# Third chunk's loads behind the second chunk's norm, rotary splits written in runs, zeros from all partitions, scale sums and masks later: one encoder layer on one core

## The chip, the cores and the metric

The kernel runs on one core of one Trainium2 chip. The core has a matrix engine (TensorE, PE in the profile), a vector engine (VectorE, DVE), a scalar engine (ScalarE, ACT), GpSimd (POOL) and SyncE (SP), which here only issues transfers between the chip's memory and the core's on-chip buffers; GpSimd issues some transfers too. The metric is the device time of one launch in microseconds. The kernel before took 2810.66 us, the median of three runs (2803.78, 2810.66 and 2811.31).

## The reference

One layer of an encoder for 2048 tokens of width 1024: a normalised input is projected to queries, keys, values and a gated branch; banded attention at three dilations and a gated depthwise convolution run side by side; then cross-attention over 256 memory rows and a squared-ReLU MLP with 4096 hidden columns. All inputs are float32. Cut to what matters here:

```python
y = rmsnorm(h, norm_mix_g[l]) @ w_in[l]                    # 1024 -> 3*512 + 2*512
q = partial_rotary(y[..., 0:D_ATT].reshape(B, S, 8, 64))   # first 16 of 64 columns turned
k = partial_rotary(y[..., D_ATT:2 * D_ATT].reshape(B, S, 8, 64))
v = y[..., 2 * D_ATT:3 * D_ATT].reshape(B, S, 8, 64)
att = dilated_sliding_attention(q, k, v).reshape(B, S, D_ATT)
conv = conformer_conv(a, g, ...)                           # a * sigmoid(g), 31 taps, layernorm, silu
h = h + jnp.concatenate([att, conv], axis=-1) @ w_out[l]
...                                                        # cross-attention over mem
u = rmsnorm(h, norm_mlp_g[l]) @ w_up[l]
h = h + jnp.square(jax.nn.relu(u)) @ w_down[l]
return rmsnorm(h, norm_final_g)
```

## The kernel before

**Stage 1** is the part that the prediction speaks of most: the norm of the input and the first projections, the first 400 us or so. A product of two float32 matrices is made of three products of halves: each operand is split into a high part in float16 (a cast) and a low part (the operand less its high part), and mm3 (L269 to L272) runs high times high, high times low and low times high into one accumulator. Weights are split the same way by scaled_split (L224 to L227): ACT multiplies by a power of two (L225) and casts (L226), and VectorE or GpSimd subtracts (L227).

The 2048 tokens come in four chunks of 512. For each chunk n, xprep (from L396) does the following. It loads four tiles of 128 tokens in two halves each (xn, eight transfers, from SP for chunks 0 and 1 and from GpSimd's queue for 2 and 3). ACT squares and sums them (sumsq, L381). Then rstd_col and newton_rsqrt make the reciprocal root: VectorE adds the epsilon (L243, st_v), GpSimd takes a power (L247, rsx), VectorE does one Newton step (L248 to L250). TensorE spreads the four columns to all partitions (rb, L255), and ACT copies that (rbs, L404). Then for each of eight column blocks TensorE transposes four tiles (xt, L409), VectorE copies the block and applies gain and norm (xv, L416), ACT casts it to the high half (xh, L417) and GpSimd subtracts for the low half (xl, L418). The un-normalised transpose goes to a scratch (xscr) through SP.

Beside it run the projections: glu_first (columns g and a of blocks 0 and 1, for chunks 0 and 1; sig at L667 is their gate, flo_a and flo_g the low halves of their weights), glu (the other blocks), lin_qk for queries and keys, and lin_v for values. lin_qk is called with "r" for the rotary columns, sixteen per head and eight heads, which are gathered in the order h, x, j (head, half, index) and written to the split weights in the order x, j, h; lraw_qr and lraw_kr are those weights in float32, lwhi and lwlo their halves (L818, L819). Their product is turned by VectorE and GpSimd (rope, sw) and split again (sth, stl, L878, L879). vscale loads each block of v's columns in two halves (vsq), squares them on ACT (L697), adds on GpSimd (L698, L699) and sums over partitions on TensorE (vss, L706), for a power-of-two scale. qkscale does the like for q and k with ACT (qks, L773). lin_v loads its weights (raw_v) and scales them (L729). memory transposes the 256 memory rows (mt, L440) and splits them on ACT and VectorE (mhi L446, mlo L447). edges writes zeros around v's scratch (vtok) and the convolution's scratch (uscr). Later, Matrices.back evicts a block of a matrix for the cross-attention out of the accumulators (eb, L578), scaled by a column.

**What sets the order.** The pieces are Python generators. weave steps a main one and, by a rate, side ones (L98); pinned and behind run a step as if it were issued right after an instruction that was recorded in the dictionary last under a name, by tc.issue_after (L78 to L96): "x1_7" is the cast of the second chunk's last high half, "xl0_7" the first chunk's last low half, "xs1" and "xs3" the last scratch store of chunks 1 and 3, "pe" the last matmul, "dve" the last recorded operation of VectorE. The framework then sorts each engine's queue by these positions. An engine runs its queue in order. SP's queue holds most transfers; each of its issues also waits, by a semaphore, for the transfer that was issued eight before it.

Of the kernel before, what the change touches and what calls it, by code (L numbers as in the profile page):

```python
# [12 lines left out]
F16 = mybir.dt.float16  # L13
BF16 = mybir.dt.bfloat16
I32 = mybir.dt.int32
AF = mybir.ActivationFunctionType
# [5 lines left out]
P = 128  # L22
S = 2048
D = 1024
H = 8
# [22 lines left out]
def hybrid_layer(ctx, tc, A, out):  # L48
# [7 lines left out]
    def dma(o, i, q=None):  # L56
        return (q or nc.sync).dma_start(o, i)  # L57
# [166 lines left out]
    def scaled_split(raw, c, hi, lo, eng):  # L224
        ACT.activation(raw, raw, AF.Copy, scale=c)  # L225
        last["split"] = ACT.copy(hi, raw)  # L226
        eng.tensor_tensor(lo, raw, hi, op=ALU.subtract)  # L227

# [17 lines left out]
    def newton_rsqrt(dst, v, t):  # L246
        POOL.tensor_tensor(dst, v, mhalf.to_broadcast([P, v.shape[1]]), op=ALU.pow)  # L247
        DVE.tensor_tensor(t, dst, dst, op=ALU.mult)  # L248
        DVE.scalar_tensor_tensor(t, t, -0.5, v, op0=ALU.mult, op1=ALU.mult)
        return DVE.scalar_tensor_tensor(dst, t, 1.5, dst, op0=ALU.add, op1=ALU.mult)  # L250
# [145 lines left out]
    def xprep(sp, n):  # L396
        xtiles(n)
        nat = [load_nat(sp, A["x"][0, 512 * n + P * j:512 * n + P * (j + 1), :], f"xn{n}_{j}", q=nc.gpsimd if n > 1 else None) for j in range(4)]
        yield
        r = yield from rstd_nat(sp, nat, f"x{n}", n == 1)  # L400
        rb = ps("c", f"rb{n}")
        last[f"rbt{n}"] = bcast_rows(rb, r, 4)
# [52 lines left out]
    class Matrices:  # L455
# [108 lines left out]
        def back(self, i):  # L564
# [5 lines left out]
            for mc in range(2):  # L570
# [6 lines left out]
                ev = zp.tile([P, 512], F32, tag=f"z{(2 * i + mc) % 8}", name=f"eb{h}{mc}{nh}")  # L577
                ACT.activation(ev, pt, AF.Copy, scale=rmem[:, mc:mc + 1])  # L578
                dma(bscr[4 * nh:4 * nh + 4, :, 2 * h + mc, :].rearrange("m p c -> p m c"),
# [110 lines left out]
    def vscale():  # L690

        for pr in range(4):
# [7 lines left out]
            yield  # L700
            yield
            with ExitStack() as st:
                after(st, "pe", "dve")
# [9 lines left out]
    def lin_v(hook):  # L713
# [4 lines left out]
        def load(e):  # L718
            raws[e] = wp.tile([P, 8, P], F32, tag="raw", name=f"raw_v{e}", bufs=2)
            with ExitStack() as st:  # L720
                after(st, "pe", "xs3")
                dma(raws[e], wcols(w_in, 2 * DATT + P * e))
# [23 lines left out]
        for t in range(4 * NG):  # L746
# [4 lines left out]
            for k in range(KC):  # L751
# [7 lines left out]
                                                   op1=ALU.subtract)  # L759
            dma(vtok[256 + P * t:256 + P * (t + 1)], st.rearrange("p h e -> p (h e)"))  # L760
            if t % 2:
# [36 lines left out]
    def lin_qk(isq, c):  # L798
# [5 lines left out]
        if c == "r":  # L804
# [9 lines left out]
            for x in range(2):  # L814
                rv = raw.rearrange("p k (h x j) -> p k h x j", x=2, j=8)[:, :, :, x, :]
                hv = hi[:, :, x * 64:(x + 1) * 64].rearrange("p k (j h) -> p k h j", h=H)
                lv = lo[:, :, x * 64:(x + 1) * 64].rearrange("p k (j h) -> p k h j", h=H)
                ACT.copy(hv, rv)  # L818
                DVE.tensor_tensor(lv, rv, hv, op=ALU.subtract)  # L819
# [97 lines left out]
    def edges():  # L917
        zrow = wp.tile([16, 1, VR], F16, tag="raw", name="zrow", bufs=2)
        DVE.memset(zrow, 0.0)
        zb = zrow.to_broadcast([16, 16, VR])  # L920
        for t0 in (0, 256 + S):
            dma(vtok[t0:t0 + 256].rearrange("(q x) e -> q x e", q=16), zb)
        for c in range(4):
            dma(uscr[c][:, 0:15], zero[:, 0:15])
            dma(uscr[c][:, 15 + S:2080], zero[:, 0:17])

    with ExitStack() as st:
# [40 lines left out]
        next(x1)  # L968
        next(four)
        early01 = (0, 1)  # L970
        units = [four] + [u for c in range(2, 4) for u in glu(c, early01)]
# [15 lines left out]
        mem = memory(sp)  # L987
        later = pinned(chain(xprep(sp, 2), islice(mem, 1), xprep(sp, 3), mem), "x1_7", "xl0_7")
        qks = pinned(qkscale(), "x1_7", "xs1")
# [22 lines left out]
    with ExitStack() as st0:  # L1012
        after(st0, "pe", "xs3")
        dma(mask, A["masks"])
# [1028 lines left out]
```

## Time and profile before

The profile is of one execution, taken by the hardware profiler.

| what | value |
|---|---|
| median of three runs | 2810.66 us (2803.78 to 2811.31) |
| the profiled execution's own time | 2811.16 us |
| its span in the profile | 2809.4 us |
| mean granted clock of TensorE | 0.989 |
| transfers | 535.67 MB, 191 GB/s over the span |

The span is what the engines' records cover; the execution's own time is what the runs are compared by. "Busy" is time inside instructions. Idle time is put down to the instruction that ended it: "[3.86 <-DVE rsx L250]" says that the engine stood for 3.86 us ahead of this instruction, and that the last thing it waited for was VectorE's line 250. The granted clock is what the throttle gave TensorE, 1.00 being full speed. A name such as rsx or xh stands for a buffer, and a line "xh<-xv" for writing the one from the other; a number in a buffer's name is left out there.

### The profile page before, as it was taken

Reading aid. Unit: us, or ns where it says so; the run is one execution under the profiler, and the core shown is the slowest. Engines: PE = TensorE matmul, PEld = TensorE weight load, DVE = VectorE, ACT = ScalarE, POOL = GpSimd, SP = SyncE. Lnnn points to the kernel's source line nnn. Section 1 sums busy time; section 2 is a strip of 40 time slices with the busy share of each in tenths; the row PEclk is TensorE's granted clock in tenths of the full one; section 3 lists DMA queues with packets and bytes.
Section 4 is the critical chain, followed back from the end, with each engine's and each line's share of the span. In section 5 each row is a group of like instructions: output and inputs, shape, how many; then the busy total and the mean of one; then the engine's idle time right before and its main releaser. Section 6 shows DMA issues by size and latency. Waiting matters only on the chain.

```text
span 2809.4 us, 40570 instructions
## 1 busy us (share of the span) xinstructions
PE 2695.4 (96%) x14783; PEld 2074.4 (74%) x14783; DVE 1901.4 (68%) x3477; ACT 1271.7 (45%) x2170; POOL 587.9 (21%) x807
## 2 busy tenths in 40 slices
PE   7979999889999999999999999999999999999998
PEld 4434448776778788788788788887887788878877
DVE  5548826665689876568986478666475776566765
ACT  6742316655545333434554443454344444444435
POOL 6445403543202122300111201121010122100000
PEclk9989999999999999999999999999999999999999
DMA  6775437887835666767467867774544554584553
GB/s 237 206 196 116 133 117 203 237 243 200 270 114 178 200 218 217 241 215 216 137 187 224 251 209 216 234 231 138 170 128 131 184 196 149 179 295 153 167 184 105
DMA packets 459815, 535.67 MB, mean 191 GB/s; under 512 B 98172, under 2 KB 329200, under 8 KB 459616
## 3 DMA queue, kind: packets, MB, share of 16 engines
q1 hardware_dynamic: 420992, 406.52, 48.4%
q0 software_dynamic: 36752, 123.06, 12.5%
q10 hardware_dynamic: 1872, 3.52, 0.3%
q8 instruction: 116, 1.90, 0.3%
q14 instruction: 83, 0.68, 0.1%
HBM read 384.46 MB, written 148.52 MB: 190 GB/s over the span
## 4 chain that ended last, share of the span: by engine, by line
PE 65%; DMA 10%; issue 9%; DVE 7%; ACT 4%; SPq 3%; POOL 3%; POOLq 0%; ACTq 0%; DVEq 0%
PE b L1741 5%; PE dn L270 4%; PE dn L271 4%; PE dn L272 4%; PE up L270 3%; PE up L272 3%; PE up L271 3%; SPq L57 3%; PE lin L270 2%; PE lin L271 2%; PE lin L272 2%; PE pt L1029 2%; PE s L1222 1%; PE x L271 1%; PE x L270 1%
## 5 line engine op out<-in xcount | busy, mean ns | idle before, releaser
L287 DVE SCALAR_TENSOR_TENSOR cacc<-cu,cwu,cacc 128x512 f32<-128x512 f32 x480 | 391.7, 818 | 6.2
L1023 ACT ACTIVATE sm<-sm,o 128x256 f32<-128x256 f32 (+1 forms) x384 | 160.0, 467 | 109.6 <-DVE o L1022 109.5
L270 PE MATMUL dn<-hhh,whi_d 128*128 128x512 f32 x512 | 201.9, 404 | 3.0 <-ACT hhh L1577 1.7
L270 PE MATMUL up<-mh,whi_u 128*128 128x512 f32 x512 | 203.9, 398 | 0.0
L271 PE MATMUL dn<-hhl,whi_d 128*128 128x512 f32 x512 | 200.0, 393 | 0.8 <-DVE hhl L1578 0.8
L272 PE MATMUL up<-mh,wlo_u 128*128 128x512 f32 x512 | 200.0, 391 | 0.0
L271 PE MATMUL up<-ml,whi_u 128*128 128x512 f32 x512 | 199.7, 390 | 0.0
L272 PE MATMUL dn<-hhh,wlo_d 128*128 128x512 f32 x512 | 198.9, 391 | 0.0
L1022 DVE CUSTOM_DVE_ANT_0 sm<-s,mask 128x256 f32<-128x256 f32 (+1 forms) x384 | 126.8, 374 | 35.8 <-PE s L1222 16.1
L1033 DVE TENSOR_TENSOR pl<-pt,ph 128x512 f16<-128x512 f32 x160 | 109.6, 686 | 48.6 <-ACT ph L1032 48.1
L247 POOL TENSOR_TENSOR nr<-st_v,mhalf 128x4 f32<-128x4 f32 x12 | 13.5, 1126 | 597.3 <-DVE st_v L243 597.3
L1592 DVE TENSOR_TENSOR h<-h,dn 128x512 f32<-128x512 f32 x128 | 86.3, 683 | 70.1 <-PE dn L272 69.5
L1032 ACT CAST ph<-pt 128x512 f16<-128x512 f32 x160 | 92.5, 578 | 79.3 <-PE pt L1029 78.5
L270 PEld LDWEIGHTS dn<-hhh,whi_d 128*128 128x128 f32 x512 | 95.3, 188 | 22.4 <-ACT hhh L1577 3.5
L272 PEld LDWEIGHTS up<-mh,wlo_u 128*128 128x128 f32 x512 | 96.1, 188 | 20.4
L272 PEld LDWEIGHTS dn<-hhh,wlo_d 128*128 128x128 f32 x512 | 96.2, 188 | 20.2
L271 PEld LDWEIGHTS dn<-hhl,whi_d 128*128 128x128 f32 x512 | 96.4, 188 | 19.4 <-DVE hhl L1578 1.7
L271 PEld LDWEIGHTS up<-ml,whi_u 128*128 128x128 f32 x512 | 96.3, 188 | 18.6
L270 PEld LDWEIGHTS up<-mh,whi_u 128*128 128x128 f32 x512 | 96.2, 188 | 18.6
L270 PE MATMUL o<-cath,whi_o 128*128 128x512 f32 x256 | 102.6, 402 | 5.3 <-ACT whi_o L261 4.6
L270 PE MATMUL x<-pth,whi_b 128*128 128x512 f32 x256 | 100.4, 398 | 2.4 <-ACT xp L1501 1.4
L270 PE MATMUL xs<-whi_a,yh 128*128 128x512 f32 x256 | 102.4, 401 | 0.0
(631 smaller groups left out, 7995.0 us busy)
## 6 DMA issues: line engine op xcount, KB each, us to landing
raw_u<-in_w_up_dram SPq DMA_DIRECT2D x64, 512.0 KB
raw_d<-in_w_down_dram SPq DMA_DIRECT2D x64, 512.0 KB
k<-kscr SPq DMA_DIRECT2D x32, 640.0 KB
raw_a<-ascr SPq DMA_DIRECT2D x32, 512.0 KB
raw_b<-bscr SPq DMA_DIRECT2D x32, 512.0 KB
lou<-wlo_u POOLq DMA_DIRECT2D x32, 512.0 KB, 5.5
lod<-wlo_d POOLq DMA_DIRECT2D x32, 512.0 KB, 5.8
wlo_u<-lou SPq DMA_DIRECT2D x32, 512.0 KB
```

Source lines behind the costliest of these rows:

```text
L57: return (q or nc.sync).dma_start(o, i)
L270: PE.matmul(o, lh, rh, start=first, stop=False)
L271: PE.matmul(o, lh, rl, start=False, stop=False)
L272: last["pe"] = PE.matmul(o, ll, rh, start=False, stop=end)
L287: DVE.scalar_tensor_tensor(acc, u[:, t:t + 512], cwu[:, c, t:t + 1], acc, op0=ALU.mult, op1=ALU.add)
L1022: last["dve"] = DVE.tensor_tensor_reduce(dst, so, mask[:, 256 * m:256 * m + nk], 1.0, 3e38, ALU.add, ALU.min, mn)
L1023: last["act"] = ACT.activation(dst, dst, AF.Exp, bias=mn, scale=-1.0)
L1029: last["pe"] = PE.transpose(pt[:, j, :], sm[:, j, :], ident)
L1032: ACT.copy(ph, pt)
L1033: DVE.tensor_tensor(pl, pt, ph, op=ALU.subtract)
L1592: last["dve"] = DVE.tensor_tensor(hs[m], hs[m], pt, op=ALU.add)
L1741: PE.matmul(o, w[i][:, k, :], Y[b][q][k], start=first and k + x == 0, stop=k == 3 and x == 2, skip_group_check=not first)
```

## The change

Seven edits:

1. The generator that prepares chunks 2 and 3 and the memory (later) is pinned behind the second chunk's last cast, the low half flo of the a-columns of block 1, and the last matmul, where it was pinned behind "x1_7" and "xl0_7". scaled_split records that low half, and newton_rsqrt its power (this record is not used). For chunks 2 and 3 xprep has one step more between the norm and rb.
2. Of the sixteen evictions in Matrices.back, the eight with mc = 1 go from ACT to VectorE.
3. vscale has one step more between the additions on GpSimd and the matmuls.
4. raw_v's loads are pinned behind "xs1" instead of "xs3".
5. The split of the rotary columns runs over x, j, h instead of h, x, j, so that each write goes to 64 float16 values in a row, and the reads jump.
6. The rows of zeros for vtok are read from 128 partitions, two rows from each, instead of 16 partitions with sixteen rows from each.
7. The mask's load is pinned behind the store of v's tile 7 instead of "xs3".

```diff
@@ scaled_split, newton_rsqrt
-        eng.tensor_tensor(lo, raw, hi, op=ALU.subtract)
+        last["lo"] = eng.tensor_tensor(lo, raw, hi, op=ALU.subtract)
...
-        POOL.tensor_tensor(dst, v, mhalf.to_broadcast([P, v.shape[1]]), op=ALU.pow)
+        last["pow"] = POOL.tensor_tensor(dst, v, mhalf.to_broadcast([P, v.shape[1]]), op=ALU.pow)
@@ xprep, after r = yield from rstd_nat(...)
+        if n > 1:
+            yield
@@ Matrices.back
-                ACT.activation(ev, pt, AF.Copy, scale=rmem[:, mc:mc + 1])
+                if mc:
+                    DVE.tensor_scalar(ev, pt, rmem[:, 1:2], None, op0=ALU.mult)
+                else:
+                    ACT.activation(ev, pt, AF.Copy, scale=rmem[:, 0:1])
@@ vscale, ahead of the matmuls
             yield
             yield
+            yield
@@ lin_v, load
-                after(st, "pe", "xs3")
+                after(st, "pe", "xs1")
                 dma(raws[e], wcols(w_in, 2 * DATT + P * e))
@@ lin_v, store of tile t
-            dma(vtok[256 + P * t:256 + P * (t + 1)], st.rearrange("p h e -> p (h e)"))
+            v = dma(vtok[256 + P * t:256 + P * (t + 1)], st.rearrange("p h e -> p (h e)"))
+            if t == 7:
+                last["v7"] = v
@@ lin_qk, "r"
-                rv = raw.rearrange("p k (h x j) -> p k h x j", x=2, j=8)[:, :, :, x, :]
-                hv = hi[:, :, x * 64:(x + 1) * 64].rearrange("p k (j h) -> p k h j", h=H)
-                lv = lo[:, :, x * 64:(x + 1) * 64].rearrange("p k (j h) -> p k h j", h=H)
+                rv = raw.rearrange("p k (h x j) -> p k x j h", x=2, j=8)[:, :, x]
+                hv = hi[:, :, x * 64:(x + 1) * 64].rearrange("p k (j h) -> p k j h", h=H)
+                lv = lo[:, :, x * 64:(x + 1) * 64].rearrange("p k (j h) -> p k j h", h=H)
                 ACT.copy(hv, rv)
                 DVE.tensor_tensor(lv, rv, hv, op=ALU.subtract)
@@ edges
-        zrow = wp.tile([16, 1, VR], F16, tag="raw", name="zrow", bufs=2)
+        zrow = wp.tile([P, 1, VR], F16, tag="raw", name="zrow", bufs=2)
         DVE.memset(zrow, 0.0)
-        zb = zrow.to_broadcast([16, 16, VR])
+        zb = zrow.to_broadcast([P, 2, VR])
         for t0 in (0, 256 + S):
-            dma(vtok[t0:t0 + 256].rearrange("(q x) e -> q x e", q=16), zb)
+            dma(vtok[t0:t0 + 256].rearrange("(q x) e -> q x e", q=P), zb)
@@ the weaving of stage 1
+        last["flo"] = last["lo"]
...
-        later = pinned(chain(xprep(sp, 2), islice(mem, 1), xprep(sp, 3), mem), "x1_7", "xl0_7")
+        later = pinned(chain(xprep(sp, 2), islice(mem, 1), xprep(sp, 3), mem), "x1_7", "flo", "pe")
@@ the mask's load
-        after(st0, "pe", "xs3")
+        after(st0, "pe", "v7")
         dma(mask, A["masks"])
```

What this does to the queues, at three places. First GpSimd's queue at the second chunk's norm, before (rsx is the power at L247; the xn rows are the loads of the third chunk):

```order
L418 TENSOR_TENSOR xl_0_391<-xv_7_619,xh_0_390 128x512
L57 DMA xn_0_0_911<-in_x_dram 128x512
L57 DMA xn_0_1_912<-in_x_dram 128x512
L57 DMA xn_1_0_915<-in_x_dram 128x512
L57 DMA xn_1_1_916<-in_x_dram 128x512
L57 DMA xn_2_0_919<-in_x_dram 128x512
L57 DMA xn_2_1_920<-in_x_dram 128x512
L57 DMA xn_3_0_923<-in_x_dram 128x512
L57 DMA xn_3_1_924<-in_x_dram 128x512
L247 TENSOR_TENSOR rsx_636<-st_v,mhalf 128x4
L227 TENSOR_TENSOR flo_a_675<-fraw_a_436,fhi_a_674 128x1024
L418 TENSOR_TENSOR xl_1_411<-xv_0_670,xh_1_410 128x512
```

And the same piece of GpSimd's queue with the change:

```order
L420 TENSOR_TENSOR xl_0_391<-xv_7_619,xh_0_390 128x512
L247 TENSOR_TENSOR rsx_636<-st_v,mhalf 128x4
L227 TENSOR_TENSOR flo_a_675<-fraw_a_436,fhi_a_674 128x1024
L57 DMA xn_0_0_911<-in_x_dram 128x512
L57 DMA xn_0_1_912<-in_x_dram 128x512
L57 DMA xn_1_0_915<-in_x_dram 128x512
L57 DMA xn_1_1_916<-in_x_dram 128x512
L57 DMA xn_2_0_919<-in_x_dram 128x512
L57 DMA xn_2_1_920<-in_x_dram 128x512
L57 DMA xn_3_0_923<-in_x_dram 128x512
L57 DMA xn_3_1_924<-in_x_dram 128x512
L420 TENSOR_TENSOR xl_1_411<-xv_0_670,xh_1_410 128x512
```

The power and the low half flo_a moved ahead of the eight loads, which now stand right before the second chunk's first low half.

Second, ACT's queue where the rotary columns are split, before (lraw_q is another weight tile, xh_3 the fourth chunk, mhi the memory's high half):

```order
L818 CAST lwhi_kr<-lraw_kr 128x8x8x8 x2
L417 CAST xh_3_1192<-xv_4_1449 128x512
L417 CAST xh_3_1192<-xv_5_1461 128x512
L417 CAST xh_3_1194<-xv_6_1473 128x512
L225 ACTIVATE lraw_q_1779<-lraw_q_1779,qkc 128x1024
L417 CAST xh_3_1194<-xv_7_1522 128x512
L818 CAST lwhi_qr<-lraw_qr 128x8x8x8 x2
L446 ACTIVATE mhi_1529<-mt_1533,gm 128x256
```

And with the change:

```order
L826 CAST lwhi_kr<-lraw_kr 128x8x64 x2
L419 CAST xh_3_1207<-xv_4_1449 128x512
L419 CAST xh_3_1207<-xv_5_1498 128x512
L419 CAST xh_3_1209<-xv_6_1510 128x512
L826 CAST lwhi_qr<-lraw_qr 128x8x64 x2
L225 ACTIVATE lraw_q_1779<-lraw_q_1779,qkc 128x1024
L419 CAST xh_3_1209<-xv_7_1571 128x512
L448 ACTIVATE mhi_1578<-mt_1582,gm 128x256
```

The casts of lwhi have another shape, and those of qr moved ahead of the scaling of lraw_q and of one cast of the fourth chunk.

Third, SP's queue behind the writes of zeros, before (vsq are the two halves of v's first block):

```order
L57 DMA rope_kr_1789<-in_rope_dram 128x512
L57 DMA lraw_k_1964<-in_w_in_dram 128x8x16
L57 DMA lraw_k_1964<-in_w_in_dram 128x8x48 x2
L57 DMA vsq_1824<-in_w_in_dram 128x4x128
L57 DMA lraw_k_1964<-in_w_in_dram 128x8x16
L57 DMA raw_v_2655<-in_w_in_dram 128x8x128
L57 DMA raw_v_2657<-in_w_in_dram 128x8x128
L57 DMA mask<-in_masks_dram 128x1664
L57 DMA vsq_1825<-in_w_in_dram 128x4x128
L57 DMA cu_0_1832<-uscr_70 128x542
```

And with the change:

```order
L57 DMA rope_kr_1789<-in_rope_dram 128x512
L57 DMA vsq_1824<-in_w_in_dram 128x4x128
L57 DMA lraw_k_1964<-in_w_in_dram 128x8x16
L57 DMA lraw_k_1964<-in_w_in_dram 128x8x48 x2
L57 DMA lraw_k_1964<-in_w_in_dram 128x8x16
L57 DMA vsq_1825<-in_w_in_dram 128x4x128
L57 DMA raw_v_2640<-in_w_in_dram 128x8x128
L57 DMA rope_kr_1834<-in_rope_dram 128x512
L57 DMA cu_0_1832<-uscr_70 128x542
```

The second vsq moved ahead of raw_v; one raw_v is gone from here to a place some 70 rows earlier (behind the first two qks loads), and the mask to one some 80 rows later.

## The prediction, made before the changed kernel was run

> **What bounds the kernel now.** I read the page first: engine totals, then the span in 40 slices.
>
> ```profile
> PE 2695.4 (96%) x14783; PEld 2074.4 (74%) x14783; DVE 1901.4 (68%) x3477; ACT 1271.7 (45%) x2170; POOL 587.9 (21%) x807
> PE   7979999889999999999999999999999999999998
> ```
>
> TensorE is busy for 96% of 2809.4 us, and its thin slices are the first and the third (70 us each), in stage 1. A saving must take idle time from TensorE, so I next asked for its busy time and granted clock by stretches (columns: stretch, its length, then busy us of PE, PEld, DVE, ACT, POOL with counts, the granted clock, DMA share, GB/s).
>
> ```profile
> 40.00:250.00 210.00, 184.09 (x857) 89.78 (x855) 118.64 (x188) 107.65 (x188) 104.00 (x104) 0.92 0.70 184
> 250.00:415.00 165.00, 165.00 (x770) 75.52 (x769) 106.41 (x137) 35.82 (x47) 54.54 (x73) 1.00 0.42 116
> 45.00:50.00 5.00, 4.41 (x15) 1.99 (x16) 1.78 (x5) 3.69 (x7) 1.17 (x2) 0.66 0.10 36
> 80.00:90.00 10.00, 8.23 (x27) 3.20 (x27) 2.87 (x6) 10.00 (x24) 6.94 (x5) 0.66 0.58 183
> 145.00:155.00 10.00, 7.13 (x27) 3.90 (x28) 6.56 (x11) 4.97 (x9) 5.96 (x14) 0.66 0.87 193
> 175.00:185.00 10.00, 8.64 (x27) 3.85 (x28) 2.61 (x4) 5.68 (x8) 7.96 (x7) 0.60 0.44 99
> 210.00:225.00 15.00, 11.64 (x44) 5.09 (x42) 14.89 (x14) 6.73 (x10) 12.83 (x14) 0.77 0.59 148
> ```
>
> From 250 to 415 us TensorE has no gap; from 40 to 250 it has 210 − 184.09 = 25.9 us of them, at a mean clock of 0.92. The timeline of TensorE says where (start, duration, instruction; in brackets the idle time before it and who ended it).
>
> ```profile
> 45.59 0.62 PE L255 MATMUL rb<-ident,rsx 128*128 128x128 f32 x4 [3.86 <-DVE rsx L250]
> 79.41 0.65 PE L255 MATMUL rb<-ident,rsx 128*128 128x128 f32 x4 [2.27 <-DVE rsx L250]
> 81.83 0.59 PE L270 MATMUL lin<-xh,lwhi_g 128*128 128x512 f16 x1 [1.77 <-ACT sig L667]
> 147.87 1.94 PE L440 MATMUL mt<-ident,mn 128*128 128x128 f32 x8 [5.52 <-DVE mlo L447]
> 176.25 1.01 PE L706 MATMUL vss<-ones,vsq 128*128 128x1 f32 x4 [6.15 <-POOL vsq L699]
> 208.57 0.38 PE L270 MATMUL lin<-xh,lwhi_k 128*128 128x512 f16 x1 [2.36 <-DVE rope_qr L866]
> 214.90 1.01 PE L706 MATMUL vss<-ones,vsq 128*128 128x1 f32 x4 [3.36 <-POOL vsq L699]
> ```
>
> These seven sum to 25.3 us. Behind the long ones the clock drops: what a stretch loses on top of its idle time is about (1 − clock) × busy time, so 0.34 × 4.41 = 1.5 us at 45, 0.34 × 8.23 = 2.8 at 80, 0.34 × 7.13 = 2.4 at 145, 0.40 × 8.64 = 3.4 at 175, 0.23 × 11.64 = 2.7 at 210: 12.8 us. So some 38 us in five places are on offer in stage 1, and each edit is weighed against the place it touches.
>
> **The change part by part.** I number the five places.
>
> **Place 1, the second chunk's norm (45.59).** What the late transposes waited for, on GpSimd and its neighbours:
>
> ```profile
> 36.58 3.76 POOL L57 DMA_DIRECT2D xn<-in_x_dram  x7
> 36.71 0.17 DVE L243 TENSOR_SCALAR st_v<-ssx 128x4 f32<-128x4 f32 x1
> 41.89 1.04 POOL L247 TENSOR_TENSOR rsx<-st_v,mhalf 128x4 f32<-128x4 f32 x1
> 38.59 1.05 ACT L226 CAST fhi_a<-fraw_a 128x1024 f16<-128x1024 f32 x1
> 42.91 2.11 POOL L227 TENSOR_TENSOR flo_a<-fraw_a,fhi_a 128x1024 f16<-128x1024 f32 x1
> 53.74 0.38 PE L271 MATMUL lin<-xl,lwhi_g 128*128 128x512 f16 x1
> 64.91 1.61 POOL L57 DMA_DIRECT2D xn<-in_x_dram  x3 [2.37 <-PE xt L409]
> ```
>
> The variance is there at 36.88, but the power at L247 begins at 41.89: eight load issues of the third chunk stand before it on GpSimd, 5 us. The changed kernel puts them behind the power and behind flo_a. The power can then run at 36.9 and rsx is ready about 5 us earlier, which covers the 3.86 us stall, and the 1.5 us of clock go with it: 5.3. What is late next: the eight issues (3.76/7 = 0.54 each, 4.3 in all) now stand between flo_a and the second chunk's first xl. flo_a would end near 41.8 (ACT's cast fhi_a ends at 39.64, then 2.11), the issues near 46.2, and the first xl near 47.3; its reader, at 53.74 now, comes about 6 us earlier, at 47.7. The cover is 0.4 us. I take **5.3**, bounds 0 (all given back) and 5.4.
>
> The rows give 0.54 us for each of these loads, at 36.58 and again at 64.91 (1.61/3), and the sum goes by that. [...]
>
> **Place 2, the third chunk's norm (79.41 and 81.83).** ACT's timeline:
>
> ```profile
> 73.65 0.63 ACT L773 ACTIVATE qks<-qks 128x512 f32<-128x512 f32 x1 [0.87 <-DMA qks<-in_w_in_dram]
> 81.10 0.68 ACT L667 ACTIVATE sig<-lin,wscl 128x512 f32<-128x512 f32 x1
> ```
>
> ACT's squares of the third chunk are mixed with squares of q and k columns that wait for their transfers, and behind them comes sig. In the changed order more of the chunk's squares precede the waiting ones, and one square, not eight, stands ahead of the cast and sig. The extra yield puts rb only two matmuls later. Of 2.27 + 1.77 + 2.8 = 6.8 I leave about 2 us of wait, since the loads start later too; a 2.36 us wait (208.57) is too short to have cost clock. I take **4.8**, bounds 0 and 6.8.
>
> **Place 3, rotary splits before mem's transposes (147.87).**
>
> ```profile
> 137.72 1.15 ACT L225 ACTIVATE lraw_q<-lraw_q,qkc 128x1024 f32<-128x1024 f32 x1 [2.35 <-DMA lraw_q<-in_w_in_dram]
> 139.28 4.71 ACT L818 CAST lwhi_qr<-lraw_qr 128x512 f16<-128x512 f32 x2
> 141.78 4.67 DVE L819 TENSOR_TENSOR lwlo_qr<-lraw_qr,lwhi_qr 128x512 f16<-128x512 f32 x2 [5.22 <-ACT lwhi_qr L818]
> 188.81 1.16 ACT L878 ACTIVATE sth_kr<-rope_kr,qkc 128x512 f16<-128x512 f32 x1
> 152.91 1.08 DVE L879 SCALAR_TENSOR_TENSOR stl_kr<-rope_kr,qkc,sth_kr 128x512 f16<-128x512 f32 x1 [1.04 <-ACT sth_kr L878]
> ```
>
> A cast that writes single f16 values 16 bytes apart takes 4.71/2 = 2.36 us, the subtraction 2.34. In the changed form writes run in 64s and only the reads jump. No row has this form; the nearest, also 512 elements a partition with strided f32 reads and f16 runs, are sth_kr at 1.16 and stl_kr at 1.08. Bounds 1.1 and 2.36; I take 1.15. The qr pair then costs 2.3 on each engine instead of 4.7, and its casts stand ahead of lraw_q instead of behind it, so that neither its 2.35 us wait nor its 1.15 us delays them: mlo can be 4.8 us earlier by the casts and some 3.5 by the order, against a stall of 5.52. With 2.4 of clock I take **8**, bounds 3 (if the casts cost what they did) and 8.
>
> **Place 4, the first sums of v's columns (176.25).** The chain of waits and SP's queue:
>
> ```profile
> 139.11 12.99 SPq L57 DMA_DIRECT2D uscr<-zero  x8
> 162.22 2.08 SPq L57 DMA_DIRECT2D raw_v<-in_w_in_dram  x2
> 164.35 1.16 SPq L57 DMA_DIRECT2D mask<-in_masks_dram  x1
> 165.61 7.74 DMA vsq<-in_w_in_dram
> 142.00:148.00 6.00, 0.48 (x3) 0.16 (x2) 5.85 (x6) 3.81 (x6) 0.11 (x1) 0.79 0.90 100
> 156.00:160.00 4.00, 4.00 (x20) 1.77 (x19) 0.00 (x0) 0.00 (x0) 0.00 (x0) 1.00 1.03 390
> ```
>
> The eight tiny zero transfers hold SP for 12.99 us, because an issue waits for the transfer eight before it and the two large writes of zeros (520 KB each, 16 partitions) move at 100 GB/s: 1.065 MB / 100 GB/s = 10.6 us. From 128 partitions they could move at the 390 GB/s seen at 156, 2.7 us; bounds 2.7 and 10.6, and I take the fast end, since wide reads are what reached 390. That brings SP forward by about 8 us. Behind it, one raw_v (512 KB), the other raw_v and the mask (832 KB) no longer stand ahead of the second vsq, whose issue at 165.61 and landing 7.74 later end the wait; it now follows lraw_k directly. I estimate landing at 152 to 156 on the old scale instead of 173.4, and the matmuls stand 24 matmuls (5.2 us) later on TensorE. Stall 6.15 and clock 3.4 could go whole; since lraw_k and the ropes remain ahead, I take **8** of 9.6, bounds 0 and 9.6.
>
> The rows leave open whether the 100 GB/s come from the few partitions or from writing the same zeros again and again. [...]
>
> **Place 5, 208.57 and 214.90.** The same chain one turn later: GpSimd works off what the late vsq had held up, and the rotary work and the second sums wait for it. These sums go from matmul 816 to 875 of the order, and their loads are ahead of time. Of 2.36 + 3.36 + 2.7 = 8.4 I take **6.5**, bounds 0 and 8.4.
>
> **The evictions of the matrices, and the loads made later.**
>
> ```profile
> L578 ACT ACTIVATE eb<-pb,rmem x16: 687/688/698, 684.6 to 722.1; 128x512 f32<-128x512 f32 x16
> 684.00:723.00 39.00, 29.62 (x163) 22.59 (x161) 13.42 (x30) 21.68 (x35) 15.90 (x21) 0.90 0.94 322
> L1022 DVE CUSTOM_DVE_ANT_0 sm<-s,mask x384: 273/415/426, 439.3 to 1869.4; 128x256 f32<-128x256 f32 x128, 128x128 f32<-128x128 f32 x64
> L729 DVE TENSOR_TENSOR raw_v<-raw_v,vbc x4: 1212/1214/1222, 294.6 to 318.2; 128x1024 f32<-128x1024 f32 x4
> ```
>
> Eight evictions of 0.688 us leave ACT for VectorE, 5.5 us, at about the same price. In the stretch where they lie ACT is busy 21.7 of 39 us and VectorE 13.4, but the DMA share is 0.94, so most of TensorE's gaps there are the transfers'. I take **1.2**, bounds −1 and +3. The mask is first read at 439.3, and its new place, behind the store of v's eighth tile, lies between the last of raw_v's products (318.2) and that, with the transfers at a share of 0.42 from 250 to 415: 0. raw_v is first read at 294.6; its early copy moves 512 KB ahead of q and k squares that place 2 has let wait, at most 2.2 us of transfers there, which is within that place's bounds.
>
> **Sum.** 5.3 + 4.8 + 8 + 8 + 6.5 + 1.2 = 33.8. Every stage-1 chain is tight, and what was hidden behind one stall stands bare when it goes: I take off 5, two new waits of the 2.4 us kind seen at 208.57. That leaves 29: 2811.16 − 29 = **2782 us**. The profiled execution lies 0.5 above the median of 2810.66 (2803.78 to 2811.31), so the sum needs no shift.
>
> **Rivals.** First, *the queue does not help*: the zeros stay slow, or vsq is late behind lraw_k all the same. For it: vsq took 7.74 us to land although only 256 KB, and the share is 1.03 already at 156. Against it: 1.35 MB leave its front. Then places 4 and 5 keep their 18 us and only two thirds of the rest stays, 5.3 + 4.8 + 8 + 1.2 − 2 = 17: **2794**. Second, *the change does nothing that can be told*: stalls move with the work, as each chain ends in the same matmuls; for it speaks that rb's second wait ends with ACT, which is busy 10.00 of 10 us at 80 to 90; against it, that there is no wait from 250 to 415 which could take them up. About 2808. Third, *slower*: GpSimd's eight issues at their new place take far longer than 0.54, and hold up both the second chunk's xl and the third chunk's loads. It decides from the point where the issues take the 0.4 us of cover plus the whole gain of 29, that is over 4.2 us each in place of 0.54. At 5 us each they take 40, 36 more than now: TensorE stands some 35 us and loses 2.8 of clock, against 29 gained: 38 − 29 = 9 slower, **2820**. The quoted rows speak against it, with 0.54 at both places.
>
> **How the numbers follow.** My forecast has 0.69, the queue's rival 0.20, no change 0.06, slower 0.05. About 0.3% (8.4 us) is what a measurement of this kernel can tell from no change; 2782 and 2794 are both beyond it, so faster 0.89, same 0.06, slower 0.05. The range: full removal of all bounds, 5.4 + 6.8 + 8 + 9.6 + 8.4 + 3 = 41, gives 2770 below; above, the first rival with place 2 gone too gives 17 − 4.8 = 12, 2799. So 2770 to 2799 holds some 8 in 10.
>
> **What would show it.** Place 1: the power starts within 1 us of st_v, and eight issues behind flo_a at about 0.54. Place 2: rb2's wait under 2.3, no sig wait. Place 3: casts of lwhi_qr near 1.15 us and no wait of mt on mlo. Place 4: SP's eight small zeros take some 4 us instead of 12.99, transfers near 390 GB/s, and vss waits for nothing. Place 5: no clock below 1.00 from 175 to 250. TensorE's idle time between 40 and 250 should fall from 25.9 to about 8 us. I am wrong if xl becomes the wait at 47, if the f16 casts stay above 2 us, so that ACT keeps place 3, or if vsq still lands last.

## The result, and the profile after

The changed kernel takes 2782.68 us, the median of six runs (2778.42 to 2786.64), beside 2810.98 us for six runs of the kernel before (2803.78 to 2817.11). The ratio is 0.990, with a 95% interval of 0.9882 to 0.9918: 23 to 33 us less. The profiled execution of the changed kernel took 2778.42 us, the lowest of its six; its span is 2776.6 us. It was a lucky one, and its stage 1 is the earliest of the three executions that are compared below.

Engine totals and the span in 40 slices, from the page of the changed kernel:

```profile
PE 2686.4 (97%) x14783; PEld 2073.0 (75%) x14783; DVE 1905.0 (69%) x3485; ACT 1261.7 (45%) x2162; POOL 588.0 (21%) x807
PE   7999999998999999999999999999999999999998
```

TensorE's busy time fell by 9 us too, with the same 14783 instructions; its mean granted clock is 0.993 where it was 0.989. The stretch that carried the sum, in the changed kernel, and two pieces of it that are used further on:

```profile
40.00:250.00 210.00, 201.87 (x989) 99.79 (x987) 139.20 (x210) 107.99 (x196) 120.75 (x128) 0.98 0.72 193
46.00:62.00 16.00, 16.00 (x89) 8.92 (x88) 9.07 (x18) 5.12 (x9) 11.00 (x13) 1.00 0.70 254
190.00:200.00 10.00, 10.00 (x42) 4.27 (x41) 9.82 (x11) 6.20 (x9) 9.57 (x10) 0.87 0.41 112
```

Idle time in these 210 us fell from 25.9 to 8.1 us. What the clock lost, (1 − clock) × busy time, fell from 0.08 × 184.09 = 14.7 to 0.02 × 201.87 = 4.0. Together 28.5 us. Now the first product of v's tiles, the first row of the stage in which TensorE has no gap, before and after:

```profile
330.44 0.38 PE L270 MATMUL v<-wvh,xh 128*128 128x512 f16 x1
```

```profile
301.89 0.38 PE L270 MATMUL v<-wvh,xh 128*128 128x512 f16 x1
```

That is 28.55 us earlier. The two executions differ by 32.7 us as a whole (2811.16 and 2778.42), so the other 4 us came behind this row, where stage 1 has no part. This row is the measure of the experiments: it holds what stage 1 gave and nothing of the noise behind it. One execution of each kernel stands behind the 28.55; over three executions of the changed stage 1, further on, it is 26.5, beside 28.3 for the medians.

Of the seven long waits three are left. TensorE's timeline of the changed kernel, the waits of more than 1 us between 40 and 250 us:

```profile
75.03 0.38 PE L270 MATMUL lin<-xh,lwhi_g 128*128 128x512 f16 x1 [3.81 <-ACT sig L672]
76.69 1.11 PE L255 MATMUL rb<-ident,rsx 128*128 128x128 f32 x4 [1.06 <-DVE rsx L250]
...
189.30 0.58 PE L270 MATMUL lin<-xh,lwhi_k 128*128 128x512 f16 x1 [2.30 <-DVE rope_qr L874]
```

The second chunk's rb, mt and vss no longer wait. The wait of lin on sig has doubled, from 1.77 to 3.81. The moved pieces at work, first on GpSimd, then on ACT, SP and TensorE:

```profile
36.78 1.03 POOL L247 TENSOR_TENSOR rsx<-st_v,mhalf 128x4 f32<-128x4 f32 x1 [0.31 <-DVE sqv_a L214]
39.53 2.13 POOL L227 TENSOR_TENSOR flo_a<-fraw_a,fhi_a 128x1024 f16<-128x1024 f32 x1 [1.72 <-ACT fhi_a L226]
41.60 4.32 POOL L57 DMA_DIRECT2D xn<-in_x_dram  x8
```

```profile
127.78 2.05 ACT L826 CAST lwhi_qr<-lraw_qr 128x512 f16<-128x512 f32 x2
129.51 6.15 SPq L57 DMA_DIRECT2D uscr<-zero  x8
144.34 0.63 ACT L702 ACTIVATE vsq<-vsq 128x512 f32<-128x512 f32 x1 [3.25 <-DMA vsq<-in_w_in_dram]
149.49 0.63 ACT L702 ACTIVATE vsq<-vsq 128x512 f32<-128x512 f32 x1 [0.50 <-DMA vsq<-in_w_in_dram]
160.57 0.50 PE L712 MATMUL vss<-ones,vsq 128*128 128x1 f32 x4
```

The power begins at 36.78 instead of 41.89, the eight issues take 0.54 us each at their new place, a cast takes 1.03 us, SP's eight small zeros 6.15, and the second vsq is squared at 149.49 where it landed at 173.35 before.

### The profile page after: what moved, and what is told of

It reads as the page before. It is cut to its first block, busy times and chain, and to the rows that moved or that the text cites. A ratio compares the mean times of both kernels' runs of the same rounds, so it can differ in the third digit from the quotient of the medians.

```text
span 2776.6 us, 40568 instructions
## 1 busy us (share of the span) xinstructions
PE 2686.4 (97%) x14783; PEld 2073.0 (75%) x14783; DVE 1905.0 (69%) x3485; ACT 1261.7 (45%) x2162; POOL 588.0 (21%) x807
## 4 chain that ended last, share of the span: by engine, by line
PE 69%; DMA 9%; issue 8%; DVE 7%; ACT 3%; POOL 3%; SPq 2%; ACTq 0%; POOLq 0%; DVEq 0%
PE b L1750 7%; PE dn L270 4%; PE dn L271 4%; PE dn L272 4%; PE up L270 3%; PE up L272 3%; PE up L271 3%; PE lin L270 2%; PE lin L272 2%; PE lin L271 2%; PE pt L1038 2%; SPq L57 2%; PE s L1231 2%; PE x L271 1%; PE x L270 1%
## 5 line engine op out<-in xcount | busy, mean ns | idle before, releaser
L247 POOL TENSOR_TENSOR nr<-st_v,mhalf 128x4 f32<-128x4 f32 x12 | 13.5, 1126 | 596.4 <-DVE st_v L243 596.4
L271 PE MATMUL o<-catl,whi_o 128*128 128x512 f32 x256 | 101.0, 395 | 1.7 <-DVE catl L1181 1.7
```

The costliest lines, as they stand in the source:

```text
L271: PE.matmul(o, lh, rl, start=False, stop=False)
```

## The experiments

Where a kernel undoes a part, it starts from the changed kernel; "alone" starts from the kernel before. The measure is the start of v's first product (330.44 before, 301.89 changed).

**How far one stage 1 differs from itself.** The changed kernel again, unaltered:

> The changed kernel once more, unaltered, as the measure for the others on the same chip. Its first profile had the lowest time of six, and the runs that share its stage 1 had v's first product at 306.0 and 306.2 instead of 301.9. If that profile was the odd one: v's first product at 304 to 307 and a wait of lin on sig of 4.2 to 5.2 us. If it was typical: 301 to 303. The ratio to the kernel before again 0.988 to 0.992.

```profile
77.03 0.59 PE L270 MATMUL lin<-xh,lwhi_g 128*128 128x512 f16 x1 [5.01 <-ACT sig L672]
191.13 0.38 PE L270 MATMUL lin<-xh,lwhi_k 128*128 128x512 f16 x1 [1.44 <-DVE rope_qr L874]
...
303.70 0.38 PE L270 MATMUL v<-wvh,xh 128*128 128x512 f16 x1
```

2784.31 us (2777.95 to 2790.89), ratio 0.9901 with 0.9881 to 0.9920. v's first product at 303.70, between my two guesses. A third execution of the same stage 1 comes from this edit, which undoes the evictions only:

```diff
-                if mc:
-                    DVE.tensor_scalar(ev, pt, rmem[:, 1:2], None, op0=ALU.mult)
-                else:
-                    ACT.activation(ev, pt, AF.Copy, scale=rmem[:, 0:1])
+                ACT.activation(ev, pt, AF.Copy, scale=rmem[:, mc:mc + 1])
```

> The changed kernel with all sixteen evictions on ACT. Stage 1 is the changed kernel's, so v's first product tells how far the same stage 1 differs from run to run: 301.9 to 304. From the first pb product to the last it took 34.9 us before and 34.4 after. If the evictions matter: 35 to 36 us. If the transfers set that stretch: 34.2 to 34.8.

It gave 306.18. So one stage 1 differs by 4.3 us between executions (301.89, 303.70, 306.18; mean 303.9), mostly in the wait on sig (3.81, 5.01, 4.73) and the waits from 160 to 230, and a difference of less than some 4 us between two single profiles is not told. The stretch of pb products took 33.6 us with all evictions on ACT (660.4 to 694.0), beside 34.4 and 33.9 in two executions of the changed kernel: no gain from moving them can be told. VectorE pays a little more for one than ACT:

```profile
L583 ACT ACTIVATE eb<-pb,rmem x8: 667/688/692, 653.5 to 684.7; 128x512 f32<-128x512 f32 x8
L581 DVE TENSOR_SCALAR eb<-pb,rmem x8: 750/751/752, 654.9 to 688.6; 128x512 f32<-128x512 f32 x8
```

(The columns are minimum, median and maximum in ns, and the first and last start.) The single time of this run, 2795.26, says little: from v's first product to pb's it took 354.2 us, where the other executions of the changed kernel and of its variants took 348 to 356.

**Place 1, undone and alone.**

```diff
@@ third chunk's pin undone
-        if n > 1:
-            yield
...
-        later = pinned(chain(xprep(sp, 2), islice(mem, 1), xprep(sp, 3), mem), "x1_7", "flo", "pe")
+        later = pinned(chain(xprep(sp, 2), islice(mem, 1), xprep(sp, 3), mem), "x1_7", "xl0_7")
```

> The changed kernel with the third chunk's loads pinned as before and without xprep's extra step. My theory of place 1: the eight load issues stand ahead of the power again, rb of the second chunk waits about 3.9 us and the clock drops behind it, so the first product of v's tiles, at 301.9 us in the changed kernel, starts 4 to 6 us later, at 306 to 308, less up to 1 us if place 2 gets better by its old order. The rival: the power's place is worth nothing, because the low half flo or the loads set the pace anyway; then 301.9 within 1 us.

TensorE's timeline of that kernel:

```profile
46.36 1.09 PE L255 MATMUL rb<-ident,rsx 128*128 128x128 f32 x4 [3.73 <-DVE rsx L250]
81.48 0.65 PE L255 MATMUL rb<-ident,rsx 128*128 128x128 f32 x4 [2.30 <-DVE rsx L250]
83.90 0.59 PE L270 MATMUL lin<-xh,lwhi_g 128*128 128x512 f16 x1 [1.77 <-ACT sig L670]
...
202.33 0.42 PE L270 MATMUL lin<-xh,lwhi_k 128*128 128x512 f16 x1 [3.87 <-DVE rope_qr L872]
```

v's first product at 315.89, 12.0 later than the mean of 303.9: more than place 1, and twice what was expected. The rb wait is back as foretold, the old form of place 2 with it (2.30 + 1.77), and the rotary products wait 1.43 us at 165 and 3.87 at 202. Idle time and clock together, place 1 lost 6.6 us (40 to 64 us), the rotary products 4 to 5 us more than in the three executions, and place 2 (64 to 100 us) about what it lost there, 6.9 beside 6.4 to 8.4. The mt wait did not return. The same edit alone, made on the kernel before:

> The kernel before with the third chunk's loads behind the second chunk's norm and xprep's extra step, and nothing else. Place 1 by my theory: the power at 36.8, no wait of rb on rsx at 41 to 46, eight issues of 0.54 us behind flo, xl ready in time. Place 2 by what the changed kernel showed: a wait of lin on sig of 3 to 5.5 us in place of 1.77. In sum v's first product 4 to 8 us before 330.4. The rival: the 5 us of place 1 stand at mlo or vss again, whose chains this doesn't touch, and v's first product is within 3 us of 330.4.

```profile
132.50 4.76 ACT L820 CAST lwhi_qr<-lraw_qr 128x512 f16<-128x512 f32 x2
...
76.62 0.59 PE L270 MATMUL lin<-xh,lwhi_g 128*128 128x512 f16 x1 [4.67 <-ACT sig L669]
141.28 1.06 PE L442 MATMUL mt<-ident,mn 128*128 128x128 f32 x8 [0.74 <-DVE mlo L449]
166.00 1.01 PE L708 MATMUL vss<-ones,vsq 128*128 128x1 f32 x4 [7.25 <-POOL vsq L701]
208.26 1.01 PE L708 MATMUL vss<-ones,vsq 128*128 128x1 f32 x4 [5.64 <-POOL vsq L701]
```

v's first product at 323.02, 7.4 earlier. Place 1 is cured (no wait of rb between 40 and 64 us), place 2 has the new long wait on sig, and place 3 is nearly cured as well (5.52 to 0.74) although the casts still take 2.38 us each: this edit is what moves lwhi_qr ahead of lraw_q on ACT. What was saved ahead of vss stands partly in front of it (6.15 to 7.25, 3.36 to 5.64).

**Place 3, the form of the rotary split, undone and alone.**

```diff
-                rv = raw.rearrange("p k (h x j) -> p k x j h", x=2, j=8)[:, :, x]
-                hv = hi[...].rearrange("p k (j h) -> p k j h", h=H)
+                rv = raw.rearrange("p k (h x j) -> p k h x j", x=2, j=8)[:, :, :, x, :]
+                hv = hi[...].rearrange("p k (j h) -> p k h j", h=H)
```

> The changed kernel with the rotary split's old form (h, x, j); every queue keeps its order. My theory of place 3, that the price of the casts counts: four casts near 2.36 us instead of 1.03, four subtractions near 2.34 instead of 1.0, mlo 3 to 5 us later, a wait of mt on mlo of 1 to 4 us, and v's first product 2 to 6 us later than 301.9. The rival, that the order of ACT's queue alone cured place 3: the casts cost 2.36 but no wait comes back, 301.9 within 1 us.

```profile
132.25 4.76 ACT L826 CAST lwhi_qr<-lraw_qr 128x512 f16<-128x512 f32 x2
...
141.00 1.06 PE L442 MATMUL mt<-ident,mn 128*128 128x128 f32 x8 [0.70 <-DVE mlo L449]
161.15 0.38 PE L270 MATMUL lin<-xh,lwhi_qr 128*128 128x512 f16 x1 [2.68 <-DVE rope_kr L874]
```

With the old form and the new order mt waits 0.70 us only, less than the 1 to 4 I gave. v's first product at 310.05, 6.1 later, comes with a wait of 2.68 us behind it, at a rotary product of q; with its clock that wait cost 4.3 us (150 to 180 us). So the form is worth something here too, at another place. And the new form with the old order:

> The kernel before with the rotary split in the new form and nothing else; ACT's queue keeps its old order, with the waiting lraw_q ahead of lwhi_qr. If the price of the casts is place 3: the casts take 1.03 us, mlo comes 3.5 to 5 us sooner, mt's wait falls from 5.52 to under 2, and v's first product is 4 to 8 us before 330.4. If the order is needed too (lraw_q's transfer holds the casts): a wait of 2.5 to 4.5 us stays and v's first product is 1 to 3.5 us before 330.4.

```profile
133.46 1.15 ACT L225 ACTIVATE lraw_q<-lraw_q,qkc 128x1024 f32<-128x1024 f32 x1 [2.12 <-DMA lraw_q<-in_w_in_dram]
135.03 2.03 ACT L818 CAST lwhi_qr<-lraw_qr 128x512 f16<-128x512 f32 x2
...
172.19 1.02 PE L706 MATMUL vss<-ones,vsq 128*128 128x1 f32 x4 [10.79 <-POOL vsq L699]
```

Here lraw_q still waits for its transfer ahead of the casts, and yet mt does not wait at all. v's first product at 323.72, 6.7 earlier, with vss's wait grown from 6.15 to 10.79. So the form and the order each cure place 3 without the other; with both, one of them is idle there.

**Place 4, the zeros, undone and alone, and from 32 partitions.**

```diff
-        zrow = wp.tile([P, 1, VR], F16, tag="raw", name="zrow", bufs=2)
+        zrow = wp.tile([16, 1, VR], F16, tag="raw", name="zrow", bufs=2)
...
-        zb = zrow.to_broadcast([P, 2, VR])
+        zb = zrow.to_broadcast([16, 16, VR])
```

> The changed kernel with the zeros written from 16 partitions; SP's order is kept. My theory of place 4: SP's eight small zeros take about 13 us instead of 6.15, vsq lands some 7 us later, and vss or the rotary products wait again, v's first product 3 to 8 us later than 301.9. The rival, that moving raw_v, the mask and vss out of the way was enough: vsq lands 7 us later too, but the sums were ready 8 us ahead of vss, so no wait and 301.9 within 1 us.

```profile
132.91 15.25 SPq L57 DMA_DIRECT2D uscr<-zero  x8
...
156.21 0.63 ACT L702 ACTIVATE vsq<-vsq 128x512 f32<-128x512 f32 x1 [11.76 <-DMA vsq<-in_w_in_dram]
160.87 1.15 ACT L225 ACTIVATE lraw_k<-lraw_k,qkc 128x1024 f32<-128x1024 f32 x1 [3.66 <-DMA lraw_k<-in_w_in_dram]
163.90 0.58 ACT L872 COPY sw_kr<-lin 64x512 f32<-64x512 f32 x1 [1.37 <-POOL vsq L703]
...
165.85 0.59 PE L270 MATMUL lin<-xh,lwhi_qr 128*128 128x512 f16 x1 [6.93 <-DVE rope_kr L874]
```

v's first product at 313.51, 9.6 later. The wait has another name: vss stands late enough on TensorE not to wait, but a rotary product waits 6.93 us for VectorE's rope_kr, which waits for ACT's copy sw_kr. ACT's rows show the link: it stands 11.76 us at the first square of vsq, whose load is late (3.25 in the changed kernel), then 3.66 at lraw_k (2.52 there), and sw_kr stands behind both on its queue. Only 1.37 us of sw_kr's delay is a wait for GpSimd's addition of vsq, as in the changed kernel (1.38); vsq and sw share one ring of buffers (t2), which would explain it, but no run tests that. The zeros alone, on the kernel before:

> The kernel before with the zeros read from 128 partitions and nothing else. If the zeros set place 4: SP's eight small zeros take about 6 us instead of 12.99, vsq lands some 7 us sooner, vss's 6.15 us wait goes nearly whole with its clock, and v's first product comes 6 to 10 us before 330.4. If raw_v and the mask ahead of vsq hold it anyway (1.35 MB, some 3.5 us at 390 GB/s): a wait of vss of 3 to 5 us stays, and v's first product is 1 to 4 us before 330.4.

```profile
138.95 5.72 SPq L57 DMA_DIRECT2D uscr<-zero  x8
...
200.97 0.59 PE L270 MATMUL lin<-xh,lwhi_k 128*128 128x512 f16 x1 [3.20 <-DVE rope_qr L866]
207.30 0.61 PE L706 MATMUL vss<-ones,vsq 128*128 128x1 f32 x4 [2.06 <-POOL vsq L699]
```

v's first product at 320.08, 10.4 earlier, the largest part of the three edits made alone, though not by more than single profiles differ. The first vss does not wait, with raw_v and the mask still ahead of the second vsq, so that the transfers in front of it are not what held it.

```diff
-        zrow = wp.tile([P, 1, VR], F16, tag="raw", name="zrow", bufs=2)
+        zrow = wp.tile([32, 1, VR], F16, tag="raw", name="zrow", bufs=2)
```

(and eight rows from each of them)

> The changed kernel with the zeros read from 32 partitions, eight rows from each. SP's eight small zeros took 12.99 to 15.25 us with 16 partitions and 6.15 with 128. If the number of partitions sets the rate (100 GB/s from 16, so some 200 from 32): 1.065 MB in 5.3 us instead of 10.6, the small zeros 7.5 to 10 us. If only the writing of the same lines counted, and the 128 were lucky: 12 to 15 us. If 32 are as good as 128: 6 to 7 us.

SP's row from 32 partitions, then windows in which the zeros are written, from 32 and from 128 (the last two columns are the transfer engines' share and the GB/s of all transfers in the window):

```profile
131.69 8.39 SPq L57 DMA_DIRECT2D uscr<-zero  x8
```

```profile
134.00:137.00 3.00, 3.00 (x17) 1.63 (x16) 1.84 (x4) 2.38 (x6) 1.14 (x2) 1.00 0.90 198
```

```profile
129.00:132.00 3.00, 3.00 (x17) 1.68 (x16) 1.89 (x2) 2.65 (x4) 0.42 (x2) 1.00 1.04 391
```

100 GB/s from 16 partitions, 198 from 32 and 391 from 128, at transfer shares of 0.90, 0.90 and 1.04. The same rows are written in all three, so the writing of the same zeros is not what set the rate. The last figure is an upper bound for the zeros: that window moved 1.17 MB, more than their 1.065. How often each partition is read changes along with their number (16, 8 and 2 rows from each), and no run separates the two. Twice the partitions gave twice the rate from 16 to 32, and four times as many, from 32 to 128, at most twice again. At 304.16 v's first product does not tell 32 partitions from 128.

**Place 2, which went the other way.** First the early raw_v, undone:

```diff
-                after(st, "pe", "xs1")
+                after(st, "pe", "xs3")
                 dma(raws[e], wcols(w_in, 2 * DATT + P * e))
```

> The changed kernel with raw_v's loads pinned behind the fourth chunk's stores as before. Place 2 went otherwise than I forecast: sig waits 3.8 us because ACT stood 3.1 us for the first q and k columns. Theory A: the early raw_v, 512 KB right behind the first two of these loads, shares the transfer engines with them; without it they land 1.5 to 3 us sooner, the wait of lin on sig falls under 2.5 us, and v's first product comes 1 to 3 us earlier than 301.9, less what raw_v costs at its old place. Theory B: they land late because SP issues them late and the fourth chunk's loads go beside them; raw_v has nothing to do with it, sig waits 3.5 to 4 us as before, and 301.9 within 1 us.

SP's and ACT's timelines in the changed kernel, and then in this one:

```profile
61.65 1.07 SPq L57 DMA_DIRECT2D qks<-in_w_in_dram  x2
...
68.58 0.63 ACT L781 ACTIVATE qks<-qks 128x512 f32<-128x512 f32 x1 [3.13 <-DMA qks<-in_w_in_dram]
74.30 0.68 ACT L672 ACTIVATE sig<-lin,wscl 128x512 f32<-128x512 f32 x1
```

```profile
62.13 2.54 SPq L57 DMA_DIRECT2D qks<-in_w_in_dram  x5
...
69.86 0.63 ACT L781 ACTIVATE qks<-qks 128x512 f32<-128x512 f32 x1 [3.93 <-DMA qks<-in_w_in_dram]
```

ACT stands 3 to 4 us at the first square of q and k with or without the early raw_v; v's first product at 306.00 lies within the spread of the changed kernel. So raw_v's place is worth nothing that can be told, there or further on. SP issues these loads at 61.65 in the one and 62.13 in the other, and ACT starts the square 7 to 8 us later (5.4 before). In seven executions, the changed kernel's two and five of its variants, lin's wait on sig is 0.6 to 0.7 us longer than ACT's stand at that square: 3.13 and 3.81 here, 4.40 and 5.01 in the changed kernel again, 4.60 and 5.21 with the zeros from 16 partitions. What lies behind ACT's standing square is the rest of the third chunk's squares, the cast and sig. The test is to take q's and k's squares out of that stretch:

```diff
-        weave(islice(steps, 34), (later, 0.4), (qks, 0.2))
+        weave(islice(steps, 10), (later, 0.4))
+        weave(islice(steps, 24), (later, 0.4), (qks, 0.283))
```

> The changed kernel with qkscale woven in from the eleventh step on, at a rate of 0.283 instead of 0.2 from the first, so that no square of q and k columns stands among the third chunk's squares on ACT. Theory B of place 2 (ACT stands 3 to 4.6 us for the first q and k columns, which land 7 us after their issue whether raw_v is early or not, and sig and the chunk's norm stand behind): the wait of lin on sig falls from 3.8 to 5.2 us to under 1.5, rb's is under 1.5, the clock holds in that stretch, and v's first product starts 3 to 6 us before 301.9 to 306; the median is 2 to 7 us under 2782.7. The rival: the fourth chunk's squares, which stand ahead of sig too, or the later scale of q and k wait in their place, and v's first product stays within 1.5 us of 301.9.

```profile
72.85 0.38 PE L270 MATMUL lin<-xh,lwhi_g 128*128 128x512 f16 x1 [0.45 <-ACT sig L672]
154.18 0.38 PE L270 MATMUL lin<-xh,lwhi_qr 128*128 128x512 f16 x1 [1.90 <-DVE rope_kr L874]
160.97 0.38 PE L270 MATMUL lin<-xh,lwhi_qr 128*128 128x512 f16 x1 [1.12 <-DVE rope_kr L874]
189.87 0.38 PE L270 MATMUL lin<-xh,lwhi_k 128*128 128x512 f16 x1 [2.84 <-DVE rope_qr L874]
```

The wait on sig is gone (0.45), although as many squares stand ahead of sig on ACT as in the changed kernel, eleven. So the standing at the load is the cause, and not the number of the squares. But v's first product stands at 302.62, 1.3 before the mean of 303.9: the rotary products wait 1.90 + 1.12 us where the changed kernel did not wait. Beside the changed kernel on the same chip:

> The kernel with q's and k's squares woven in from the eleventh step, beside the changed kernel on the same chip. Theory B of place 2: no wait of sig, v's first product 2 to 5 us ahead of the changed kernel's, and the ratio to the kernel before lower by 0.0007 to 0.002. The rival: what place 2 gives is taken by the rotary products' waits at 154 to 208, and the two ratios agree within 0.0005.

2781.11 us (2780.24 to 2782.68), ratio 0.9892 with 0.9874 to 0.9910; in its first run 0.9878 with 0.9853 to 0.9903. v's first product at 302.19. It is faster than the kernel before. That it beats the changed kernel, whose ratio measured beside it is 0.9901 with 0.9881 to 0.9920, is not told: the two intervals lie over each other. So the rival of both expectations, that other waits take what place 2 gives, can't be excluded, and the 3 to 6 us first expected did not come.

## Why the prediction was right, point by point

The forecast of 2782 us met 2782.68. The sum had 33.8 − 1.2 − 5 = 27.6 us for stage 1, and the trace shows 28.5 there (26.5 over three executions); TensorE's idle time between 40 and 250 us was to fall to about 8 us, and it is 8.1. Term by term, in the two profiles, idle time and clock together:

- **Place 1: 5.3 predicted.** The 3.86 us wait and its clock are gone, 3.86 + 0.11 × 16 = 5.6 by the stretch from 46 to 62 us, whose granted clock was 0.89 (the row below) and is 1.00. The power came 5.1 us earlier, xl in time at 45.94. The third rival's mechanism, that GpSimd's issues take far longer at their new place, did not come true: 4.32 us for eight in the changed kernel and 4.34 with the pin alone, 0.54 each. The stretch before:

```profile
46.00:62.00 16.00, 16.00 (x78) 8.16 (x77) 7.77 (x16) 8.26 (x14) 8.55 (x10) 0.89 0.44 144
```

- **Place 2: 4.8 predicted, nothing found that can be told.** This is the step that failed: "In the changed order more of the chunk's squares precede the waiting ones". Only one more does (four instead of three), and behind the second waiting one stand four squares ahead of the cast and sig, not one (eight before). The first waiting one still stands in the middle of them, its square begins 6.9 us after its issue (5.4 before), and all that comes behind it on the same queue, sig above all, got later relative to a TensorE that was now 5 to 6 us earlier. Before, 2.27 + 1.77 us; after, 3.81 + 1.06. Idle time and clock from 64 to 100 us lost 6.9 us before and 6.4, 8.4 and 8.1 in three executions after. I had counted how many instructions stand ahead of sig, and not asked whether the one that waits for a transfer moves with the rest. Taking it out of the way removed the wait.
- **Place 3: 8 predicted, and 8.4 found,** with half of the reason. 5.52 us of waiting, 0.5 beside it and 2.4 of clock went. The estimate of 1.15 us for a cast was near (1.03). But I added the effect of the form (4.8) and of the order (3.5); either alone removes the mt wait, all but 0.7 us, and the old order with the new form shows that lraw_q's transfer held nothing decisive. The lower bound of 3, for casts as dear as before, was too low for this wait.
- **Place 4: 8 predicted, 9.6 found.** The fast end of the bound was the right one: up to 391 GB/s. The prediction left open whether the 100 GB/s came from the few partitions or from the same rows written again; 198 GB/s from 32 partitions and up to 391 from 128, for the same rows, speak against the second. SP's hold was 6.15 us rather than 4. The zeros alone give 10.4, and raw_v's move nothing that the runs can tell. The mask's move and vscale's extra step were not undone in any run, so what they give is not shown.
- **Place 5: 6.5 predicted, 4.5 found.** The rotary product still waits 2.30 us at 189 (1.44 in the second execution), with a clock of 0.87 behind it: 2.30 + 0.13 × 10 = 3.6, and 0.3 before 190, are left of 8.4. The clock was not to fall below 1.00 there, and it did; the prediction took a wait of 2.36 us as too short to cost clock (1.00 behind it, from 208 to 212 us in the kernel before), and this one is shorter. The prediction saw GpSimd's work behind this place. What is left ends on VectorE's queue: it does not stand idle ahead of rope_qr (188.57), but two steps of the convolution run there at 2.15 us each, where the ones at 179 to 183 us took 0.73 to 0.75:

```profile
184.35 4.29 DVE L287 SCALAR_TENSOR_TENSOR cacc<-cu,cwu,cacc 128x512 f32<-128x512 f32 x2
```

GpSimd works without a gap beside them (3.00 of 3 us from 186 to 189); whether that is what slows them, no run tests.

- **Evictions: 1.2 predicted, nothing told.** Their cost of 0.69 became 0.75, and the stretch took 34.9 us before, 34.4 and 33.9 after, and 33.6 with all of them on ACT.
- **The discount of 5 us** for new waits was an allowance and not a mechanism. It happened to stand for place 2's 4 to 5 and place 5's 2, less what place 4 gave above 8. So the total was right partly by luck: misses of both signs met.

The rivals. The first has two slips in its working that decide nothing: its 17 us keep nine tenths of the rest, not two thirds, and with both raw_v and the mask 1.9 MB left the front of vsq, not 1.35. The queue did help, so the first fell, and its price if the zeros had stayed slow shows at 313.51 in the run that undoes them, 9.6 us of stage 1. The stalls did move with the work in the runs with one edit alone (vss 6.15 to 10.79, or to 7.25; with the zeros, rope_qr 2.36 to 3.20), which is the second rival's mechanism, but v's first product still came 6.7 to 10.4 us earlier each time. The slower case needed issues above 4.2 us, and its 5 us each were assumed; they took 0.54.

The parts come near the whole: zeros alone 10.4, pin alone 7.4, rotary alone 6.7 make 24.5, and all edits 26.5 by the mean of three executions (330.44 − 303.9). Undone one at a time they cost 9.6, 12.0 and 6.1, 27.7. One execution of each stands behind these, so 3 to 4 us of any of them are open, and how exactly they add is not shown.

## What to carry to other kernels

Ask of a queue not how many instructions stand ahead of the one that is late, but whether one of them waits for a transfer: moving everything else forward only lengthened the stop here (ACT's stand at the first square of q and k went from 2.34 to 3.13 us). When an engine's stall has two possible cures, test each without the other: at place 3 either removed the stall, and the second had nothing left to take there. And a change that removes one of several stalls in a row shows part of its worth as a longer wait at the next one (vss 6.15 to 10.79 us with the rotary form alone); count it at a row behind them all.

## What the runs showed of the hardware

A cast of 512 elements a partition from float32 to float16 took 0.6 us with runs on both sides (xh, 0.60 and 0.62), 1.03 with reads 64 bytes apart and writes in runs (2.05 for two), and 2.36 to 2.38 with reads in runs of 32 bytes and single writes 16 bytes apart (4.71 and 4.76 for two). Reads that jump, with writes in runs, cost less than twice as much here (1.03 beside 0.62); writes that jump, with reads in short runs, about four times (2.36 beside 0.62).

The zeros moved at 100, 198 and up to 391 GB/s from 16, 32 and 128 partitions, and SP, which issues eight transfers of 7.5 or 8.5 KB behind them, stood there for 12.99 to 15.25 us (the kernel before, and the changed one with 16), 8.39 (with 32) and 5.72 to 6.24 (the zeros alone, the changed kernel, and the changed kernel again).

The length of TensorE's wait alone did not tell whether clock was lost behind it. The granted clock was 0.50 from 189.8 to 192 us, behind a wait of 2.30 us (the changed kernel), and 0.50 from 215 to 220 behind 3.36 us (the kernel before). It was 1.00 from 208 to 212 behind 2.36 us (the kernel before). Behind 2.84 us (q's and k's squares later), 3.19 (the same kernel again) and 2.99 us (all evictions on ACT) TensorE's products started every 0.22 us, as they do at 1.00. What decides it is not shown.
